# Splitting the second block's first weights ahead, and loading units ahead through the regular weight tiles

## The chip, the cores and the metric

The kernel runs on one core of one Trainium2 chip. The metric is the device time of one execution in microseconds (us), the median of several runs.

## The reference

The input `x` (512 tokens of 1024 features, float32) goes through two blocks of two layers each. Everything is computed in float32.

- A layer of the first block: `x += concat(attention, HGRN, convolution) @ w_out`, where all three get their inputs from `rms_norm(x) @ w_in`; then `x += relu(rms_norm(x) @ w_mlp_in)^2 @ w_mlp_out` with 4096 hidden columns.
- A layer of the second block: `rms_norm(x) @ w_in_2` gives the inputs of four mixers (sparse attention with compressed, selected and window keys; stick-breaking attention; gated linear attention; forgetting attention) and a gate for each. `x += (sum of gate * (mixer @ w_branch_2)) @ w_out_2`; then `x += relu(rms_norm(x) @ w_ff1_2)^2 @ w_ff2_2`.

A last `rms_norm` gives the output. What matters here is that nearly all of the weights (some 16 big matrices) are read once, and that each product is float32.

## The kernel before, in words

**How a product is made.** TensorE takes `fp32r` operands. Each float32 operand is split into a high part `hi` (a rounded copy, made on ScalarE) and a low part `lo = src - hi` (made on VectorE); this is `split`, lines 316 and 317. `mm3` (lines 414 to 416) then makes three matmuls: hi with hi, hi with lo, lo with hi. The activations are split once (`xh`, `xl`); the weights are split as they come.

**How weights come.** A unit of weights is 128 partitions x 512 floats, 256 KB (`units`, line 323). `wload` (line 370) makes one unit after another: SP issues the load of the raw weights into a `wr` tile (line 384), ScalarE writes the high part into `wh`, VectorE the low part into `wl`. These three tags have a fixed number of buffers (line 110), and a tag's buffers are handed out in the order in which the code asks for them:

```python
WEIGHTS = dict(wr=4, wh=4, wl=3)
```

A unit of 512-column products costs TensorE 12 matmuls. `tlater` and `product` use units of 4 x 128 columns, `nlater` (lines 460 to 462) units of 2 x 256 columns.

**Splitting ahead.** `split_ahead` (line 333) takes a list of weights that a later layer will ask for, cuts it into the same units as `wload`, and makes a job of each: load the raw weights into a tile `pr` of its own (line 342), split them into two tiles `pp` of tags that are free at that time, and write both parts to a buffer `parts` in HBM, issued by ScalarE (line 349). `background`, called 64 times in an MLP (after each step of its loops), starts `len(todo) / 64` jobs per call and moves the running ones on by a stage. When `wload` later finds the unit's key among those kept, it loads both parts from HBM straight into `wh` and `wl` (line 379, two transfers of 256 KB on SP); no `wr` tile and no split is used.

Before the change only the MLP of the first block's layer 0 does this: 48 units of layer 1, listed by `First.ahead` (line 1116), with raw tiles of the tag `c` and parts in the tags `hz` and `hx`. The other three MLPs have no jobs.

**The MLP** (`mlp`, line 566) has four chunks of 1024 hidden columns. In each, eight steps make hidden columns (ReLU on ScalarE, line 577; square on GpSimd, line 578; split) and eight steps make output rows (scaling on VectorE, line 588; addition to `x` on GpSimd, line 590). In the last chunk each output row is also prepared for the next layer: `xh` on ScalarE (line 511), `xl` on VectorE (line 512), its square, and the sum of squares on GpSimd (line 505).

**The start of a layer of the second block** (`Second.layer`, line 2099): the first gate column (`G[0][0]`), then `narrow` (line 1485: four groups of 32 columns, among them the forget and gate logits), then `nsa_inputs` (line 1593): two projections of compression keys and values, and `compress` (line 1549), which uses raw weights in `wr` tiles as operands, 8 times two tiles, while units of four `nlater` projections are put between. The queue of other work during the sparse attention (the remaining gates of branch 0 and the first stick-breaking projections) is paced by a credit per step.

**The order of instructions** on each engine and queue is made by the tile framework when the program is built: it takes instructions by program order, but lets a later one go first when its inputs and a buffer are ready by its own timing. So a load that has a free buffer goes out early, and a load that waits for a buffer goes in its turn.

Of the kernel before, what the change touches and what calls it, by code (L numbers as in the profile page):

```python
# [20 lines left out]
F32R = mybir.dt.float32r  # L21
# [10 lines left out]
KT = D // 128  # L32
# [129 lines left out]
class Core:  # L162
# [114 lines left out]
    def ahead(self, work, u):  # L277

        n = work.load(u + 1 + AHEAD - len(work.ws))
        if work in self.queue:  # L280
            for w in self.queue[self.queue.index(work) + 1:]:
                if n <= 0:
                    break
                n -= len(w.ws)
                if n > 0:
                    n = w.load(n)
# [46 lines left out]
    def split_ahead(self, tags, wanted, steps):  # L333


        nc, todo = self.nc, [(u, m, b) for w in wanted for u, m in self.units(*w) for b in (w[2],)]

        def job(unit, m, b):
            view = lambda t: t[:, :m * b].rearrange("p (a b) -> p a b", a=m)
            raw = view(self.t(tags[0], "pr"))  # L340
            for ap, rows, cols in unit:
                nc.sync.dma_start(raw[rows, :, cols], ap)
            yield
            hi, lo = (self.t(tag, "pp", F32R) for tag in tags[1:])
            self.split(view(hi), view(lo), raw)
            yield
            d = self.tc.dram_tile([2, 128, T], F32, name="parts")
            for i, x in enumerate((hi, lo)):
                nc.scalar.dma_start(d[i][:, :m * b], x[:, :m * b].bitcast(F32))
            self.kept[self.unit_key(unit)] = d  # L350

        self.jobs, self.running = [job(*t) for t in todo], []
        self.job_rate, self.job_credit = len(todo) / steps, 0.0
# [443 lines left out]
def weave(core, *gens, until=None):  # L797


    state = [[g, f, t] for g, f, t in gens]  # L800
    need = state[:until]
    while any(st in state for st in need):
        st = min(state, key=lambda a: a[2])
        try:
            st[2] += (next(st[0]) or 1) * st[1]
            core.step()
        except StopIteration:
            state.remove(st)
# [81 lines left out]
class First:  # L890
# [437 lines left out]
    def layer(self, l, gmlp, post):  # L1328
        K, I = self.K, self.I
        w = I["w_out"][l]  # L1330
        cv, hg, at, vi = [], [], [], []
        att = self.att(l, vi, at)
        other = dict(X="hx", near="hx", far="hp", Z="hz", acc="ha")
        slots = [lambda n: K.t(other.get(n, "h"), n), lambda n: K.t(other[n], n) if n in other else K.xtile()]
        K.share, K.pool_share = -8, 1.0
        weave(K, (self.hgrn(l, 0, vi, slots[0], hg), 1, 0), (self.hgrn(l, 1, vi, slots[1], hg), 1, 7),
              (self.conv(l, cv), 2.5, 30), (att, 1, 30), until=3)
        hg = [p for _, p in sorted(hg, key=lambda a: a[0])]
        own = [K.parts(y) for y in cv + hg]
        xs = [self.out_part(w, m, own[2:] + own[:2]) for m in range(KT)]  # L1340
        K.queue_up(xs)
        K.pace(10)
        weave(K, (att, 1, 0))
        K.drain()
        K.pool_share = 0.0
        K.out_proj(w[0:512], [K.parts(y, "h", "hx") for y in at], lambda m: K.prep(m, gmlp()))
        nxt = self.ahead(1) if l == 0 else []
        K.split_ahead(("c", "hz", "hx"), nxt, 64)
        K.mlp(I["w_mlp_in"][l], I["w_mlp_out"][l], post,
              dict(h=[("y", "a")] * 4 + [("y", "h")] * 4, r="t", s="t", o="e", r2="z"))  # L1350

# [3 lines left out]
O_Q, O_KC, O_VC, O_KS = 0, 512, 640, 768  # L1355
O_NG = 1280
O_SB = 1304
O_GQ, O_GK, O_GV, O_GA, O_GG = 2840, 3096, 3352, 3864, 3880
O_FX, O_FF, O_GATE = 4392, 5928, 5936


class Second:
# [111 lines left out]
    def rope(self, v, t, n, p=128):  # L1474
# [6 lines left out]
        nc.vector.tensor_tensor(v[:, :, 0:16], v[:, :, 0:16], C, op=ALU.mult)  # L1481
        nc.vector.tensor_tensor(v[:, :, 0:16], v[:, :, 0:16], b, op=ALU.add)


    def narrow(self, l, other):
        K, nc, I = self.K, self.K.nc, self.I
        w = I["w_in_2"][l]
        ws = K.wload([(w[:, c:c + 32].rearrange("(k p) c -> p k c", p=128), slice(None), slice(32 * i, 32 * i + 32))
                          for i, c in enumerate((O_NG, O_FF, O_GA, O_GA))], KT, 128)
        p = K.pt()  # L1490
        for k in range(KT):
            K.mm3(p, *ws[k], K.xh[k], K.xl[k], k == 0, k == KT - 1)
        z = K.evac(p, "z", name="nar")
        other.get()
        if self.C is None:
            self.constants()

        pg = K.pt("ps")
        for t in range(NT):
            nc.tensor.transpose(pg[:, t * 32:t * 32 + 32], z[0:32, t * 128:(t + 1) * 128], K.ident[0:32, 0:32])  # L1500
        gt = K.small(128, "gates", bufs=1)
        nc.vector.tensor_scalar(gt, pg[:, :128], -40.0, None, op0=ALU.max)
        K.sigmoid(gt, gt)
        gt = gt.rearrange("p (t n) -> p t n", t=NT)
        for t in range(NT):
            nc.vector.tensor_scalar(gt[:, t, 0:24:3], gt[:, t, 0:24:3], self.cmpv[:, t:t + 1], None, op0=ALU.mult)

        bf = K.small(1, "foxb", bufs=1)
        nc.sync.dma_start(bf[32:40], I["fox_b_f_2"][l].rearrange("(p o) -> p o", o=1))
        zf = K.t("e", "zf")  # L1510
        nc.vector.tensor_scalar(zf[32:40], z[32:40], bf[32:40], None, op0=ALU.add)
        ls = K.t("e", "ls")[32:40]
        K.log_sigmoid(ls, zf[32:40])
        cum = K.t("e", "cum")
        nc.vector.tensor_tensor_scan(cum[32:40], K.ones[32:40, 0:1].to_broadcast([8, T]), ls, 0.0, op0=ALU.mult, op1=ALU.add)
        cf = K.bp.tile([128, T], F32R, name="cf", tag="cf")
        nc.vector.tensor_scalar(cf, K.R, 0.0, None, op0=ALU.mult)
        nc.scalar.activation(cf[32:40], cum[32:40], AF.Copy, scale=-1.0)
        nc.vector.scalar_tensor_tensor(cf[0:8], cum[32:40], -1.0, cf[32:40].bitcast(F32), op0=ALU.mult, op1=ALU.subtract)
        nc.gpsimd.tensor_copy(cf[64:128], cf[0:64])  # L1520
        self.low = K.small(T, "low", bufs=1)
        nc.scalar.activation(self.low[0:16], z[64:80], AF.Copy)
        return gt, cf
# [575 lines left out]
    def layer(self, l, gff, post):  # L2099
        K, nc, I = self.K, self.K.nc, self.I  # L2100
        bg = K.vec(I["b_gate_2"][l], "gbias", 32)
        ys = [[] for _ in range(4)]
        mixed = [None] * KT
        G, B = zip(*(self.branch(l, n, ys[n], mixed, bg) for n in range(4)))
        sV, sZ = self.heads_inputs(l, O_SB)
        fV, fZ = self.heads_inputs(l, O_FX)
        g0, g1 = self.gla_inputs(l)
        K.pool_share = 0
        G[0][0].get()
        gt, cf = self.narrow(l, G[0][1])  # L2110
        nin = {}
        K.queue_up(G[0], sV[0], sZ[0], sZ[1])
        K.pace(130 + 18 * 1.2)
        K.pool_share = 0.0
        weave(K, (self.nsa_inputs(l, nin), 1, 0))
        K.pool_share = 0
        weave(K, (self.nsa(gt, nin, ys[0]), 1, 0))
        K.queue_up(sV[1], sZ[2], sZ[3], B[0], G[1], g0["qk"], g0["v"])
        K.pace(56, 40)
        weave(K, (self.stick(sV, sZ, ys[1]), 1, 0))  # L2120
        K.queue_up(g0["g"], g1["qk"], B[1], g1["v"], G[2], g1["g"], fV[0], fZ[0])
        K.pace(24, 20)
        weave(K, (self.gla(l, (g0, g1), ys[2]), 1, 0))
        K.queue_up(fZ[1], fZ[2], B[2], fV[1], fZ[3], G[3])
        K.pace(53, 45)
        weave(K, (self.fox(fV, fZ, cf, ys[3]), 1, 0))
        K.queue_up(B[3])
        K.drain()
        K.pool_share = 0.0
        K.out_proj(I["w_out_2"][l], [K.parts(m, "v") if i < 4 else K.parts(m) for i, m in enumerate(mixed)],  # L2130
                   lambda m: K.prep(m, gff()), kept=True)
        K.mlp(I["w_ff1_2"][l], I["w_ff2_2"][l], post,
              dict(h=[("v", "y")] * 8, r="t", s="t", o="e", r2="q"))

# [58 lines left out]
```

## Time and profile before

| what | us |
|---|---|
| median of 3 runs | 3737.83 |
| the runs | 3732.4 to 3740.15 |
| the profiled execution, its own time | 3730.05 |
| its span, first to last instruction | 3728.3 |

The profile shows one execution. PE is TensorE's matmuls, PEld its weight loads, which overlap them, DVE is VectorE, ACT ScalarE, POOL GpSimd, SP the queue that issues most transfers; a small q behind an engine's name means its sequencer. L317 is line 317 of the kernel. The ends of matmuls are modelled: a stall shorter than a matmul's modelled length shows as busy time. PEclk is the granted clock of TensorE as a share of full speed, DMA the mean busy share of the 16 DMA engines. Where a wait is put down to "issue", the profile shows nothing that the engine waited for.

### The profile page before, as it was taken

The numbers are of one execution on the slowest core, as the hardware profiler recorded it, in microseconds if no ns is written. First come the engines' busy times: TensorE is split into PE (matmuls) and PEld (weight loads), VectorE is DVE, ScalarE is ACT, GpSimd is POOL, SyncE is SP. The second block draws the span as 40 slices with busy tenths as digits, with TensorE's granted clock in tenths as the row PEclk, the third lists the DMA queues.
The fourth block names the chain that finished last, engine by engine and source line by source line (L and its number), as shares of the span: only waits on it lengthen the run. The fifth ranks groups of instructions, "written<-read, shape, count | busy, mean of one in ns | idle before, by whom it ended". The sixth has DMA issues, their size and how long they took to land.

```text
span 3728.3 us, 53465 instructions
## 1 busy us (share of the span) xinstructions
PE 3618.2 (97%) x18793; PEld 3004.0 (81%) x18793; DVE 2322.3 (62%) x4594; ACT 1901.4 (51%) x3940; POOL 892.0 (24%) x885
## 2 busy tenths in 40 slices
PE   8889999998999999999999999999999999999999
PEld 7757788896788887888788888887888888888887
DVE  8885643488543346787778753335687777874334
ACT  6576433356533343678555643333567844553333
POOL 4732222344022230001213122222001121222222
PEclk9999999999999999999999999999999999999999
DMA  4105943541133344213232333334312222233332
GB/s 129 54 12 186 343 132 98 156 132 53 58 96 98 97 119 123 57 46 74 63 74 66 77 113 97 96 98 129 93 32 71 71 66 75 62 105 94 98 97 88
DMA packets 589500, 357.00 MB, mean 96 GB/s; under 512 B 53050, under 2 KB 554416, under 8 KB 589232
## 3 DMA queue, kind: packets, MB, share of 16 engines
q1 hardware_dynamic: 571952, 322.13, 31.1%
q10 hardware_dynamic: 17280, 31.46, 2.2%
q8 instruction: 148, 2.42, 0.3%
q14 instruction: 120, 0.98, 0.1%
HBM read 317.85 MB, written 35.65 MB: 95 GB/s over the span
## 4 chain that ended last, share of the span: by engine, by line
PE 82%; DVE 4%; ACT 2%; DMA 2%; issue 1%; POOL 1%; SPq 0%; ACTq 0%; DVEq 0%; POOLq 0%
PE pm L414 21%; PE pm L416 21%; PE pm L415 21%; PE pm L461 2%; PE pm L462 2%; PE pm L460 2%; PE po L714 2%; PE pt L696 1%; PE pa L1091 1%; PE pt L2041 1%; DVE wl L317 1%; PE ps L2041 1%; PE po L1896 1%; PE ps L1206 1%; DMA wr<-in_w_in_dram 0%
## 5 line engine op out<-in xcount | busy, mean ns | idle before, releaser
L317 DVE TENSOR_TENSOR wl<-wr,wh 128x512 fp32r<-128x512 f32 x948 | 678.5, 716 | 701.5 <-issue 347.8
L316 ACT ACTIVATE wh<-wr 128x512 fp32r<-128x512 f32 x948 | 594.8, 629 | 986.6 <-PE pm L415 825.9
L414 PE MATMUL pm<-xh,wh 128*128 128x512 f32 x2160 | 855.7, 396 | 14.4 <-DVE x L1138 3.8
L416 PE MATMUL pm<-xh,wl 128*128 128x512 f32 x2160 | 850.9, 394 | 4.8 <-POOL wl L389 3.8
L415 PE MATMUL pm<-xl,wh 128*128 128x512 f32 x2160 | 848.1, 393 | 0.2 <-DVE xl L512 0.2
L414 PEld LDWEIGHTS pm<-xh,wh 128*128 128x128 f32 x2160 | 407.8, 189 | 98.9 <-DVE x L1138 4.2
L416 PEld LDWEIGHTS pm<-xh,wl 128*128 128x128 f32 x2160 | 407.6, 189 | 92.9 <-POOL wl L389 5.7
L415 PEld LDWEIGHTS pm<-xl,wh 128*128 128x128 f32 x2160 | 407.6, 189 | 82.0 <-issue 2.2
L416 PE MATMUL pm<-hid,wl 128*128 128x512 f32 x1024 | 398.7, 390 | 2.3 <-DVE wl L317 2.3
L415 PE MATMUL pm<-hid,wh 128*128 128x512 f32 x1024 | 397.9, 389 | 0.0
L414 PE MATMUL pm<-hid,wh 128*128 128x512 f32 x1024 | 396.5, 390 | 0.1
L590 POOL TENSOR_TENSOR x<-x,os 128x512 f32<-128x512 f32 x124 | 205.8, 1660 | 426.7 <-DVE os L588 425.0
L578 POOL TENSOR_TENSOR s<-r 128x512 f32<-128x512 f32 x128 | 134.5, 1051 | 577.5 <-ACT r L577 540.2
L460 PE MATMUL pm<-wh,xh 128*128 128x256 f32 x896 | 257.3, 290 | 6.6 <-ACT wh L316 4.8
L461 PE MATMUL pm<-wl,xh 128*128 128x256 f32 x896 | 257.1, 288 | 2.8 <-DVE wl L317 2.5
L462 PE MATMUL pm<-wh,xl 128*128 128x256 f32 x896 | 255.2, 286 | 0.0
L416 PEld LDWEIGHTS pm<-hid,wl 128*128 128x128 f32 x1024 | 192.2, 188 | 45.0 <-DVE wl L317 5.1
L414 PEld LDWEIGHTS pm<-hid,wh 128*128 128x128 f32 x1024 | 192.2, 188 | 40.2 <-ACT wh L316 0.5
L415 PEld LDWEIGHTS pm<-hid,wh 128*128 128x128 f32 x1024 | 192.2, 188 | 39.8
L414 PE MATMUL pm<-mxh,wh 128*128 128x512 f32 x512 | 202.1, 398 | 6.3 <-ACT mxh L316 4.1
L588 DVE TENSOR_TENSOR os<-pm,R 128x512 f32<-128x512 f32 x128 | 88.5, 692 | 189.7 <-PE pm L416 189.7
L415 PE MATMUL pm<-mxl,wh 128*128 128x512 f32 x512 | 202.0, 394 | 0.0
(621 smaller groups left out, 6698.3 us busy)
## 6 DMA issues: line engine op xcount, KB each, us to landing
wr<-in_w_in_dram SPq DMA_DIRECT2D x344, 256.0 KB
wr<-in_w_ff_dram SPq DMA_DIRECT2D x256, 256.0 KB
wr<-in_w_mlp_in_dram SPq DMA_DIRECT2D x128, 256.0 KB
wr<-in_w_mlp_out_dram SPq DMA_DIRECT2D x128, 256.0 KB
parts<-pp ACTq DMA_DIRECT2D x96, 256.0 KB
wr<-in_w_branch_dram SPq DMA_DIRECT2D x64, 256.0 KB
wr<-in_w_out_dram SPq DMA_DIRECT2D x56, 256.0 KB
wh<-parts SPq DMA_DIRECT2D x48, 256.0 KB
```

Source lines behind the costliest of these rows:

```text
L316: nc.scalar.activation(hi, src, AF.Copy)
L317: nc.vector.tensor_tensor(lo, src, (hi if hi_in is None else hi_in).bitcast(F32), op=ALU.subtract)
L414: nc.tensor.matmul(out, wh, xh, start=start, stop=False)
L415: nc.tensor.matmul(out, wh, xl, start=False, stop=False)
L416: nc.tensor.matmul(out, wl, xh, start=False, stop=stop)
L460: nc.tensor.matmul(o, self.xh[kk][:, c], h, start=f, stop=False, skip_group_check=True)
L461: nc.tensor.matmul(o, self.xh[kk][:, c], l, start=False, stop=False, skip_group_check=True)
L462: nc.tensor.matmul(o, self.xl[kk][:, c], h, start=False, stop=e, skip_group_check=True)
L578: nc.gpsimd.tensor_tensor(s, r, r, op=ALU.mult)
L588: nc.vector.tensor_tensor(s, po, R2, op=ALU.mult)
L590: (nc.vector if last and m == KT - 1 else nc.gpsimd).tensor_tensor(self.x[m], self.x[m], s, op=ALU.add)
L714: nc.tensor.matmul(*x, start=start and n == 0, stop=stop and n == len(mm) - 1, skip_group_check=True)
```

## The change

Three edits. In `split_ahead`, the job's raw tile is a `wr` tile, made by `wtile`, in place of a tile of a tag given by the caller; so the caller gives two tags, those of the parts. In `First.layer`, layer 1 now gives a list as well: that of the second block's layer 0. In `Second.layer`, layer 0 gives the list of layer 1 ahead of its MLP, with parts in the tags `g` and `z`. The new `Second.ahead` lists what a layer of the second block asks for first; `narrow_columns` is the list of `narrow`, taken out of it so that both use the same.

```diff
@@ split_ahead
         def job(unit, m, b):
             view = lambda t: t[:, :m * b].rearrange("p (a b) -> p a b", a=m)
-            raw = view(self.t(tags[0], "pr"))
+            raw = self.wtile("wr", m, b)
             for ap, rows, cols in unit:
                 nc.sync.dma_start(raw[rows, :, cols], ap)
             yield
-            hi, lo = (self.t(tag, "pp", F32R) for tag in tags[1:])
+            hi, lo = (self.t(tag, "pp", F32R) for tag in tags)
             self.split(view(hi), view(lo), raw)
@@ First.layer
-        nxt = self.ahead(1) if l == 0 else []
-        K.split_ahead(("c", "hz", "hx"), nxt, 64)
+        nxt = self.ahead(1) if l == 0 else Second.ahead(K, I, 0)
+        K.split_ahead(("hz", "hx"), nxt, 64)
@@ Second
+    @staticmethod
+    def ahead(K, I, l):
+
+        w = I["w_in_2"][l]
+        out = K.wanted(w, (O_GATE, 128)) + [Second.narrow_columns(w)]
+        out += K.wanted(w, (O_KC, 128), (O_VC, 128), (O_KS, 256), (O_KS + 256, 256), (O_Q, 256), (O_Q + 256, 256))
+        out += K.wanted(w, *((O_GATE + m * 128, 128) for m in range(1, KT)))
+        out += K.wanted(w, (O_SB + 1024, 256), (O_SB, 128), (O_SB + 512, 128), (O_SB + 128, 128), (O_SB + 640, 128))
+        return out + K.wanted(w, (O_SB + 1280, 256), *((O_SB + c, 128) for c in (256, 768, 384, 896)))
+
+    @staticmethod
+    def narrow_columns(w):
+        return [(w[:, c:c + 32].rearrange("(k p) c -> p k c", p=128), slice(None), slice(32 * i, 32 * i + 32))
+                for i, c in enumerate((O_NG, O_FF, O_GA, O_GA))], KT, 128
@@ narrow
-        ws = K.wload([(w[:, c:c + 32].rearrange("(k p) c -> p k c", p=128), slice(None), slice(32 * i, 32 * i + 32))
-                          for i, c in enumerate((O_NG, O_FF, O_GA, O_GA))], KT, 128)
+        ws = K.wload(*self.narrow_columns(w))
@@ Second.layer
+        K.split_ahead(("g", "z"), self.ahead(K, I, 1) if l == 0 else [], 64)
         K.mlp(I["w_ff1_2"][l], I["w_ff2_2"][l], post,
               dict(h=[("v", "y")] * 8, r="t", s="t", o="e", r2="q"))
```

## Rows read from the trace of the kernel before

**Rows 1.** The page: span, busy time by engine, one costly group.

```profile
span 3728.3 us, 53465 instructions
...
PE 3618.2 (97%) x18793; PEld 3004.0 (81%) x18793; DVE 2322.3 (62%) x4594; ACT 1901.4 (51%) x3940; POOL 892.0 (24%) x885
...
L590 POOL TENSOR_TENSOR x<-x,os 128x512 f32<-128x512 f32 x124 | 205.8, 1660 | 426.7 <-DVE os L588 425.0
```

**Rows 2.** Stretches: bounds, length, busy PE PEld DVE ACT POOL, PEclk, DMA share, GB/s.

```profile
356.00:718.00 362.00, 355.26 (x1551) 289.66 (x1550) 173.40 (x250) 144.35 (x249) 95.02 (x70) 1.00 0.60 189
...
1036.00:1386.00 350.00, 350.00 (x1552) 289.65 (x1551) 135.99 (x208) 123.75 (x212) 94.71 (x70) 1.00 0.36 102
1386.00:2197.00 811.00, 796.06 (x4596) 675.57 (x4595) 619.33 (x1456) 480.69 (x1101) 122.72 (x155) 1.00 0.29 77
2197.00:2547.00 350.00, 350.00 (x1551) 289.65 (x1550) 136.21 (x208) 123.94 (x212) 94.34 (x74) 1.00 0.36 104
2547.00:3362.00 815.00, 798.40 (x4596) 678.43 (x4595) 599.72 (x1340) 481.41 (x1100) 119.90 (x146) 0.99 0.29 75
3362.00:3712.00 350.00, 350.00 (x1551) 289.65 (x1550) 139.52 (x205) 117.96 (x201) 93.30 (x69) 1.00 0.32 93
```

**Rows 3.** Stretches of 50 us around the start of the first MLP.

```profile
310.00:360.00 50.00, 50.00 (x223) 39.79 (x222) 31.62 (x44) 23.70 (x40) 16.21 (x12) 1.00 0.70 213
...
360.00:410.00 50.00, 46.67 (x202) 37.60 (x202) 31.31 (x50) 28.91 (x53) 8.43 (x8) 0.97 1.05 344
410.00:460.00 50.00, 46.59 (x196) 35.78 (x195) 33.70 (x43) 19.43 (x33) 13.35 (x8) 1.00 1.04 349
```

**Rows 4.** Waits of PEld, 356 to 718: us in total, times, longest.

```profile
PEld pm L416 <- DVE wl L317: 7.6, 12, 1.4
PEld pm L414 <- ACT r L577: 3.2, 1, 3.2
```

**Rows 5.** Tiles `pr` and `pp`: ns min/median/max, first and last start in us.

```profile
L342 SPq DMA_DIRECT2D pr<-in_w_in_dram x48: 367/368/1304, 298.4 to 439.2; - x48
...
L317 DVE TENSOR_TENSOR pp<-pr,pp x48: 676/685/1783, 325.3 to 474.1; 128x512 fp32r<-128x512 f32 x48
L342 SPq DMA_DIRECT2D pr<-in_w_out_dram x8: 367/368/725, 441.5 to 464.2; - x8
...
L349 ACTq DMA_DIRECT2D parts<-pp x96: 326/327/1273, 302.7 to 475.2; - x96
```

**Rows 6.** Waits of PEld, 1386 to 1510.

```profile
PEld pm L461 <- DVE wl L317: 3.4, 5, 1.7
PEld pm L460 <- ACT wh L316: 3.2, 3, 2.1
PEld ps L1564 <- DMA wr<-in_nsa_cmp_wv_dram: 1.8, 2, 0.9
```

**Rows 7.** Waits of PEld, 2547 to 3362.

```profile
PEld pm L460 <- ACT wh L316: 3.0, 2, 1.6
PEld ps L1564 <- DMA wr<-in_nsa_cmp_wv_dram: 2.8, 3, 1.3
...
PEld pm L461 <- DVE wl L317: 1.5, 3, 0.6
...
PEld ps L1564 <- DMA wr<-in_nsa_cmp_wk_dram: 1.0, 1, 1.0
```

**Rows 8.** Groups by line, 1386 to 1510: busy us, mean ns, idle before.

```profile
L317 DVE TENSOR_TENSOR wl<-wr,wh 128x512 fp32r<-128x512 f32 x33 | 22.7, 689 | 20.2 <-ACT wh L316 9.7 <-issue 5.0 <-PE pm L461 2.4
L316 ACT ACTIVATE wh<-wr 128x512 fp32r<-128x512 f32 x33 | 20.8, 630 | 41.3 <-DMA wr<-in_w_in_dram 21.5 <-PE pm L415 10.3 <-PE pm L462 5.0
```

**Rows 9.** Waits over the whole span.

```profile
DVE wl L317 <- issue: 347.8, 213, 3.9
```

**Rows 10.** The last chunk of the second MLP as a stretch.

```profile
1343.00:1386.00 43.00, 43.00 (x191) 35.59 (x191) 20.87 (x32) 18.66 (x32) 21.41 (x14) 1.00 0.51 139
```

**Rows 11.** Waits of PEld, 718 to 830, the largest entry.

```profile
PEld ps L1206 <- issue: 2.0, 2, 1.6
```

## The prediction

> **What bounds the kernel now.** I read the busy shares first. TensorE is busy 3618.2 of 3728.3 us, no other engine above 62% [rows 1]: whatever the change moves on VectorE, ScalarE or the queues counts only where TensorE waits for it. So the second view is the stretches. Cut where the first block's attention part, its MLP, and so on begin, the span has eight stretches; the six that matter here stand in [rows 2]. Three of the four MLPs take 350 us with TensorE busy in all of it, at the full granted clock. The MLP of the first block's layer 0 (356 to 718) takes 362 us. It alone now splits weights ahead, so the 48 jobs cost 12.0 us. Its idle time is only 362 - 355.3 = 6.7 us: a short stall also stretches the matmuls around it, which the view counts as busy.
>
> The third view is where in that MLP it happens. The jobs load into tiles of their own and so are not held back: the last `pr` load is issued at 464.2 and the last write of parts at 475.2 us, although the code spreads the jobs over all 64 steps [rows 5]. From 360 to 460 the DMA engines are full (share 1.05 and 1.04, 344 and 349 GB/s) and TensorE idles 3.3 and 3.4 us. From 310 to 360, with jobs already running, the share is 0.70 at 213 GB/s and TensorE idles for nothing [rows 3]. The weight-load queue of TensorE waited 7.6 us for low halves `wl` and once 3.2 us for the ReLU that was behind them on ScalarE [rows 4]: full DMA engines deliver the regular weights late.
>
> The fourth view is the start of both layers of the second block, where the 2 x 62 units lie. There TensorE waits for exactly what the change takes away: 1386 to 1510 us for `wl` 3.4, `wh` 3.2 and for raw compression weights 1.8 [rows 6], 8.4 us in all; in layer 1, 3.0, 2.8, 1.5 and 1.0, 8.3 us [rows 7].
>
> **The change part by part.** *Loading through `wr`.* No instruction is added in the MLP of layer 0. A job's raw tile is now one of the four `wr` buffers, which regular weights take in the same order. A `wr` buffer comes free only when a split into `wh`/`wl` is done, and those come free at TensorE's pace. So jobs can't run ahead by more than a few units: 48 jobs are spread over some 350 us. The burst goes, and most of its 12.0 us. Bounds: gain 0 (the price is per job, wherever it lies) to 12.0. I take 10, since the share then is far nearer to the row of 0.70 than to those above 1.
>
> *62 more jobs in the MLP of layer 1, and 62 in the MLP of the second block's layer 0.* The lists give 2 + 2 (gate column, narrow) + 4 + 8 + 8 (KC/VC, KS, Q) + 14 (gates) + 12 + 12 (stick-breaking) = 62 units, a rate of 62/64 a step. By its keys each is what `wload` asks for later. Per job: on SP one load of raw weights (368 ns to issue; four small ones for each of the two narrow units), on ScalarE a copy of 0.63 us and two issues of parts of 0.33 us, on VectorE a subtraction of 0.69 us [rows 5, 8]. In one MLP that is 62 x 1.29 = 80 us on ScalarE beside 123.8 busy, and 43 us on VectorE beside 136.0, of 350 [rows 2]. Both have room, and TensorE has three split units ahead. Behind a job's parts write, which waits on ScalarE for VectorE's half, stand the next `wh` copies, and TensorE waits for those: a delay under a microsecond, covered by those units. On the DMA engines a job moves 256 KB in and 512 KB out: 62 x 0.786 MB in 350 us is 139 GB/s on top of 102, so 241 GB/s. By the first MLP's 0.60 for 189 GB/s [rows 2] that is an estimated share of 0.77. No row has that share with jobs evenly spread. The nearest below is 0.70 without idle, the nearest above 1.04 with idle [rows 3]. The bounds are 0 and 12.0 / 48 = 0.25 us a job, 15.5 us an MLP. I take 2 each, near the lower row.
>
> *Ends of the three MLPs.* Until now no job ran in a last chunk, where VectorE and GpSimd also prepare the next layer's input. From 1343 to 1386 us VectorE is busy 20.9 us and GpSimd 21.4, together 42.3 of 43 [rows 10]. Before many of the splits VectorE idles although all that the profile knows is ready: 347.8 us in 213 waits, 1.63 us each, about one GpSimd addition of 1.66 us [rows 1, 9]. So the two seem to take turns. Eight more subtractions there are 8 x 0.69 = 5.5 us. If they never overlap, 42.3 + 5.5 is 4.8 us more than the stretch; if they do, nothing. I take 1 us at each of the three ends.
>
> The Trainium skill has a rule here: SBUF — State Buffer, "Summary: rules for kernel authors", says that a VectorE operation with two SBUF inputs and a GpSimd operation reading SBUF fully block one another. By that rule alone the sum would have 4.8 us at each end; by the row's lower bound it has 0. The trace agrees so far as the 1.63 us go.
>
> *Splits and raw loads taken out of the second block's layers.* Each of the 62 units loses its split and its raw load and gains two loads of 256 KB straight into `wh` and `wl`. From 1386 to 1510 VectorE spends 22.7 us and ScalarE 20.8 us on 33 such splits [rows 8]. Off the waits of TensorE that buys nothing, so I count only the waits: 8.4 and 8.3 us. The compression weights also stay in `wr`, which then has four buffers for them alone. Bounds: 0 (the wait comes back under another name) to the 14.9 and 16.6 us that TensorE idles in these two parts as a whole (811 - 796.1 and 815 - 798.4) [rows 2]. I take the named waits in full.
>
> *What is late next.* A kept unit holds a `wh` and a `wl` buffer from its DMA's issue on, and there are four and three. On SP a load that waits for such a buffer holds up all behind it, the compression loads among them, and the compression matmuls wait for those. The first block's layer 1 already lives so: from 718 to 830 the largest entry in the list of the weight-load queue is 2.0 us in two waits, ended by nothing that the profile shows, and no `wh` or `wl` is in that list [rows 11]. Bounds 0 to the full 8.4; I take 1 us a layer. Moving the narrow weights' list into a function and taking the `c` tiles out of use cost nothing: no instruction changes, and no one else waits for a `c` tile in the MLP.
>
> **Sum.** -10 - 8.4 - 8.3 + 2 + 2 + 3 + 2 = -17.7 us. The profiled execution took 3730.05 us, 1.75 beyond its span, so 3712.4 in its own terms. It was quicker than all three timed runs, 7.8 us under their median of 3737.83; on the median's scale the forecast is 3720 us.
>
> **Rivals.** *The price is per job.* Point of decision: the DMA share in the MLPs. Should spread traffic at about 0.77 delay the regular weights as much as the burst did, because a job now also holds one of the four `wr` buffers that they need, then 172 jobs cost 0.25 us each: 12 + 15.5 + 15.5 = 43 us against 12 now, +31. Less 16.7 and plus 2 in the layers that is +16.3: 3754 us, slower. For it: the waits of layer 0 were on `wl`, and the `wr` reserve gets thinner. Against it: at 0.70 nothing idled [rows 3]. Chance 0.15.
>
> *The ends of the MLPs give it back.* VectorE and GpSimd strictly take turns in the last chunks, 3 x 4.8 = 14.4 us in place of 3: -17.7 + 11.4 = -6.3, 3732 us, no change that can be told. For it: the 42.3 of 43 us and the 1.63 us waits. Against it: the same stretch loses nothing on TensorE today, and the splits ahead leave slack. Chance 0.15.
>
> *More than the waits.* If MLP 0 gives back all 12.0 and each second-block part 12 us, because the VectorE chain at its start gets shorter and small stalls go with it, and nothing new is late, the time is 3737.8 - 36 = 3702 us. For it: MLP 0 lost nearly twice its idle time. Against it: much of the idle time there is behind evacuations and softmax. Chance 0.18.
>
> *The change does not do what it says* (keys differ, parts are written and never read): the MLP costs stand alone, above 3738. By reading the code every key matches. Chance 0.02.
>
> **How the numbers follow.** The forecast has 0.50. A measurement of this kernel tells about 0.2%, 7.5 us, from no change, so faster means under 3730.4 and slower over 3745.3. Faster: 0.50 + 0.18 = 0.68; same: 0.15; slower: 0.15 + 0.02 = 0.17. The range runs from just below the gain of 36 us to beyond the case of the ends, with the upper cost bounds of two or three small terms: 3700 to 3742. It leaves out the 0.17.
>
> **What would show it.** Right: all four MLP stretches at 350 to 354 us; writes of parts through the whole of three MLPs instead of ending a third of the way in; no slice with a DMA share near 1; 124 fewer subtractions into `wl` and 124 more into `pp`; waits of `pm L460` and `L461` for `wh` and `wl` gone from the starts of the second block's layers, which take about 8 us less each. Wrong: MLP stretches of 360 us or more, a first wait at the layer starts on the `parts` loads, or the second block's parts unchanged although the splits are gone.

## The result, and the profile after

The changed kernel takes 3787.01 us in the median (3781.07 to 3788.93), the kernel before 3735.43 in the same comparison: a ratio of 1.0134, 95% interval 1.0117 to 1.0152. It is slower by about 50 us, where 17.7 us less were forecast.

These are the stretches of the changed kernel's profiled execution that answer to [rows 2], in the same columns (bounds, length, busy PE PEld DVE ACT POOL, PEclk, DMA share, GB/s). The bounds have moved with the work.

```profile
357.00:709.00 352.00, 350.50 (x1551) 289.46 (x1549) 191.88 (x252) 148.20 (x255) 92.58 (x69) 1.00 0.67 207
1031.00:1409.00 378.00, 361.65 (x1555) 286.71 (x1553) 206.11 (x267) 156.63 (x269) 93.66 (x69) 1.00 0.70 220
1409.00:2223.00 814.00, 797.13 (x4596) 677.72 (x4595) 585.93 (x1398) 447.97 (x1045) 121.95 (x156) 0.99 0.35 98
2223.00:2600.00 377.00, 362.23 (x1550) 285.37 (x1549) 206.49 (x266) 156.04 (x267) 90.57 (x70) 1.00 0.71 221
2600.00:3420.00 820.00, 800.37 (x4596) 679.85 (x4595) 563.88 (x1281) 447.42 (x1043) 121.34 (x150) 0.99 0.34 95
3420.00:3770.00 350.00, 350.00 (x1551) 289.65 (x1550) 139.52 (x205) 118.01 (x201) 93.33 (x69) 1.00 0.32 93
```

Cut at the last matmul of each part, to a tenth of a us: the first MLP fell from 362.0 to 351.8, the two MLPs with 62 jobs rose from 350.0 to 377.2 and 377.3, the second block's layers rose from 811.3 to 814.3 and from 815.2 to 820.1, the first block's layer 1 from 318.0 to 322.4 and the part ahead of it by 1.6. The sum is +58; the spans differ by 57.9. The DMA share in the slow MLPs is 0.70, nowhere near 1.

What TensorE waits for in the second MLP (waits of PEld, 1031 to 1409) is no transfer and hardly a weight:

```profile
PEld pm L414 <- ACT r L577: 17.4, 24, 1.5
PEld pm L414 <- issue: 10.5, 8, 2.1
PEld pm L416 <- DVE wl L317: 2.6, 11, 0.2
```

The largest entry is the ReLU that empties one of its two `pm` banks. The 10.5 us under "issue" have no cause that the profile names; a step further down shows one such wait. The view of the job tile `pp` in the same stretch says what stood ahead. The first three rows are the job's instructions, those under "sat idle" the idle time ahead of them:

```profile
L349 ACTq DMA_DIRECT2D parts<-pp x122: 326/327/743, 1032.6 to 1404.1; - x122
L316 ACT ACTIVATE pp<-wr x61: 631/632/635, 1032.0 to 1402.7; 128x512 fp32r<-128x512 f32 x61
L317 DVE TENSOR_TENSOR pp<-wr,pp x61: 691/693/742, 1032.6 to 1403.4; 128x512 fp32r<-128x512 f32 x61
its engine sat idle before it (us, times) until:
  DMA wr<-in_w_in_dram: 142.0, 61
  ACT pp L316: 127.0, 61
```

ScalarE stood idle 142.0 us ahead of 61 copies, 2.3 us each, until the job's raw weights had landed; VectorE stood idle 127.0 us ahead of the subtractions, waiting for these copies. What comes later in the queue of either engine does not pass such an instruction. A step that makes hidden columns shows it on ScalarE: the job's copy, its two writes of parts, and the ReLU (timeline of the changed kernel; start, duration, engine, and the idle time before):

```profile
1158.47 0.63 ACT L316 ACTIVATE pp<-wr 128x512 fp32r<-128x512 f32 x1 [1.85 <-DMA wr<-in_w_in_dram]
1159.13 1.13 ACTq L349 DMA_DIRECT2D parts<-pp  x2
1160.31 0.60 ACT L577 ACTIVATE r<-pm 128x512 f32<-128x512 f32 x1 [1.20 <-DVE pp L317]
```

The ReLU stands behind the copy and also behind the second write, which waits for VectorE's half: 26 of the 32 ReLUs of this MLP waited for that, 31.3 us in all. A step that makes output rows, on ScalarE, VectorE, SP and TensorE:

```profile
1200.28 0.63 ACT L316 ACTIVATE wh<-wr 128x512 fp32r<-128x512 f32 x1 [0.17 <-issue]
1204.81 0.63 ACT L316 ACTIVATE pp<-wr 128x512 fp32r<-128x512 f32 x1 [3.90 <-DMA wr<-in_w_in_dram]
```

```profile
1200.26 2.38 DVE L317 TENSOR_TENSOR wl<-wr,wh 128x512 fp32r<-128x512 f32 x2
1205.47 0.69 DVE L317 TENSOR_TENSOR pp<-wr,pp 128x512 fp32r<-128x512 f32 x1 [2.83 <-ACT pp L316]
1206.09 0.68 DVE L588 TENSOR_TENSOR os<-pm,R 128x512 f32<-128x512 f32 x1
```

```profile
1200.97 0.37 SPq L342 DMA_DIRECT2D wr<-in_w_in_dram  x1
```

```profile
1206.91 0.47 PE L414 MATMUL pm<-hid,wh 128*128 128x512 f32 x1 [0.66 <-DVE os L588]
```

The raw load is issued at 1200.97, and ScalarE's next instruction is already its copy, which starts at 1204.81. VectorE's scaling of a finished bank (L588) comes behind the subtraction; the matmul that needs this bank then stood still 0.66 us, and its weight load shows 1.05 us under "issue".

### The profile page after: what moved, and what is told of

Read it like the earlier page. It is cut to its first block, busy times and chain, and to the rows that moved or that the text cites. A ratio compares the mean times of both kernels' runs of the same rounds, so it can differ in the third digit from the quotient of the medians.

```text
span 3786.2 us, 53904 instructions
## 1 busy us (share of the span) xinstructions
PE 3640.7 (96%) x18793; PEld 3000.6 (79%) x18793; DVE 2408.8 (64%) x4594; ACT 1901.3 (50%) x3940; POOL 885.3 (23%) x885
## 4 chain that ended last, share of the span: by engine, by line
PE 69%; DMA 12%; DVE 11%; ACT 4%; issue 2%; POOL 1%; SPq 0%; DVEq 0%; ACTq 0%; POOLq 0%
PE pm L414 16%; PE pm L416 16%; PE pm L415 16%; DMA wr<-in_w_in_dram 11%; PE pm L460 2%; PE pm L461 2%; PE pm L462 2%; ACT pp L316 2%; PE po L714 2%; DVE wl L317 2%; DVE cy L1287 1%; PE pt L696 1%; PE pa L1091 1%; PE ps L1206 1%; DVE nm L661 1%
## 5 line engine op out<-in xcount | busy, mean ns | idle before, releaser
L416 PE MATMUL pm<-xh,wl 128*128 128x512 f32 x2160 | 851.6, 394 | 14.5 <-DMA wl<-parts 9.7
L316 ACT ACTIVATE wh<-wr 128x512 fp32r<-128x512 f32 x824 | 505.5, 627 | 523.6 <-PE pm L415 371.8
L414 PEld LDWEIGHTS pm<-xh,wh 128*128 128x128 f32 x2160 | 408.0, 189 | 127.0 <-ACT r L577 23.4
L414 PE MATMUL pm<-hid,wh 128*128 128x512 f32 x1024 | 399.7, 393 | 18.3 <-DVE os L588 11.8
L317 DVE TENSOR_TENSOR pp<-wr,pp 128x512 fp32r<-128x512 f32 x172 | 124.1, 722 | 336.5 <-ACT pp L316 336.5
L316 ACT ACTIVATE pp<-wr 128x512 fp32r<-128x512 f32 x172 | 108.6, 632 | 364.6 <-DMA wr<-in_w_in_dram 354.6
```

Source lines behind the costliest of these rows:

```text
L316: nc.scalar.activation(hi, src, AF.Copy)
L317: nc.vector.tensor_tensor(lo, src, (hi if hi_in is None else hi_in).bitcast(F32), op=ALU.subtract)
L414: nc.tensor.matmul(out, wh, xh, start=start, stop=False)
L416: nc.tensor.matmul(out, wl, xh, start=False, stop=stop)
```

## The experiments

Three theories. **Theory 1:** the job's copy and subtraction wait in their queues for raw weights that have not landed, ahead of the instructions that empty TensorE's banks. **Theory 2:** the jobs' traffic delays the regular weights. **Theory 3:** VectorE and GpSimd take turns, and the added subtractions are too many. Times of parts below are cut at the last matmul of each part.

### One part alone, its opposite, and fewer jobs

Only the first edit; the two new lists are empty:

```diff
-        nxt = self.ahead(1) if l == 0 else Second.ahead(K, I, 0)
+        nxt = self.ahead(1) if l == 0 else []
...
-        K.split_ahead(("g", "z"), self.ahead(K, I, 1) if l == 0 else [], 64)
+        K.split_ahead(("g", "z"), [], 64)
```

> The jobs of layer 0 alone, loaded through wr; the two new lists are empty. In the changed kernel the first MLP took 352 us against 362 before. Theory 1 (a job's copy waits in ScalarE's queue, and its subtraction in VectorE's, for raw weights that have not landed, ahead of the ReLU and the scaling that empty TensorE's banks; it costs only where nearly every step has a job), theory 2 (traffic) and theory 3 (VectorE and GpSimd take turns) all expect the first MLP at about 352 and the other three at 350, the rest as before: some 10 us faster than before, about 3726.

Measured: 3719.11 us, ratio 0.9956 (0.994 to 0.9973). The first MLP takes 353.8, the others 350.0. The median is 14.5 us below the kernel before, of which the first MLP explains 8.2. The loading through `wr` is a gain; the loss is all in the new lists.

All jobs, but the raw tile again one of a tag of its own:

```diff
-            raw = self.wtile("wr", m, b)
+            raw = view(self.t(tags[2], "pr"))
...
-        K.split_ahead(("hz", "hx"), nxt, 64)
+        K.split_ahead(("hz", "hx", "c"), nxt, 64)
...
-        K.split_ahead(("g", "z"),
+        K.split_ahead(("g", "z", "k"),
```

> All 172 jobs, but raw weights in tiles of their own again (tag c in the first block, k in the second), so that loads run ahead of their split. Theory 1: in the MLPs with 62 jobs the waits for raw weights shorten, but the jobs bunch up and the DMA engines fill as they did in the first MLP before (12.0 us for 48 jobs): each of the two about 365, the first 362. Theory 2: the same traffic in a burst costs at least as much, 377 or more. Theory 3: the same work in a shorter time, 377 or more.

Measured: 3772.32 us, 1.0102 (1.0087 to 1.0117). The three MLPs take 361.4, 363.0 and 360.9. ScalarE idles 29.1 us ahead of the 53 copies from 1040 us on, not 142. The burst is back, as two stretches of this run's second MLP show beside one after the burst:

```profile
1095.00:1145.00 50.00, 49.14 (x216) 40.04 (x215) 36.16 (x43) 21.18 (x36) 14.20 (x9) 1.00 1.07 353
1145.00:1195.00 50.00, 47.44 (x201) 36.91 (x200) 30.01 (x42) 28.96 (x50) 8.32 (x8) 1.00 1.07 359
...
1245.00:1295.00 50.00, 50.00 (x222) 41.42 (x221) 18.75 (x29) 18.38 (x32) 11.35 (x10) 1.00 0.33 95
```

So there are two prices: 11 to 13 us for a burst, whether of 48 or 62 jobs, and 27 us for 62 spread jobs that wait. Theories 2 and 3 had both put 377 or more here.

No raw loads: each job splits a resident tile.

```diff
-            raw = self.wtile("wr", m, b)
-            for ap, rows, cols in unit:
-                nc.sync.dma_start(raw[rows, :, cols], ap)
+            raw = view(self.scales[0])
```

> The jobs load no raw weights: each splits a resident tile (the kernel leaves out reading the weights ahead, so the units kept hold other numbers). Copy, subtraction and both writes of parts stay, 62 a time; nothing is left to wait for, and a third of a job's traffic is gone. Theory 1: both long MLPs at 350 to 353, the ScalarE idle time ahead of the copies gone, 50 us faster than the changed kernel. Theory 2: two thirds of the extra traffic stay, so some two thirds of the 27 us each, 368. Theory 3: no change, 377.

Measured: 3741.79 us, ratio 1.0014 (1.0005 to 1.0024). The second MLP took 350.4, as theory 1 expects, with all 62 copies, subtractions and writes in it. The third took 369.2, close to the 368 of theory 2. With nothing to hold them back the jobs bunched in both, at 1045 to 1166 and at 2208 to 2329 us. Here are the two MLPs, and 50 us out of each bunch:

```profile
1026.00:1376.00 350.00, 350.00 (x1550) 289.53 (x1549) 180.24 (x266) 155.26 (x269) 95.66 (x70) 1.00 0.60 195
1076.00:1126.00 50.00, 50.00 (x222) 41.44 (x221) 38.09 (x52) 25.77 (x45) 14.42 (x9) 1.00 1.00 339
2189.00:2558.00 369.00, 357.89 (x1551) 289.01 (x1550) 181.86 (x267) 156.50 (x269) 96.31 (x74) 1.00 0.57 187
2239.00:2289.00 50.00, 42.57 (x167) 31.07 (x166) 33.67 (x44) 25.24 (x43) 12.43 (x8) 0.97 0.97 342
```

The first of these speaks against theory 3, since the same VectorE work cost nothing. The second shows that full DMA engines (share 1.00, 339 GB/s) alone need not cost TensorE anything. In the third MLP TensorE waited 10.4 us for `wh` and 8.2 for `wl`, but the `wh` copies themselves waited only 0.5 us for raw weights; the jobs' copies stood 18.8 us on ScalarE until an earlier job's subtraction was done (11.9 in the second MLP). So its loss is not one of late raw weights; why it came there and not in the second MLP stays open. And as the traffic had changed with the waiting, theory 2 is not yet excluded for the changed kernel.

The lists cut to 48 and, later, to 55 units:

```diff
-for b in (w[2],)]
+for b in (w[2],)][:48]
```

> The two new lists cut to their first 48 units, 0.75 jobs a step as in the first MLP; otherwise the changed kernel. Theory 1: a step's ScalarE and VectorE time with the wait then fits in the 5.4 us on average, as in the first MLP: both long MLPs 352 to 355. Theory 2 and theory 3, in proportion to the jobs: 350 + 27 x 48/62 = 371 each. The layers of the second block say whether units kept ahead gain anything there: 811 and 815 before, 814 and 820 in the changed kernel.

> The two new lists cut to 55 units, 0.86 jobs a step. At 48 units these MLPs took 352 and 350, at 62 they took 377. Theory 1 in its form with a threshold (per step ScalarE's or VectorE's work, waits included, against 5.4 us of TensorE's): a few us, 353 to 364. If something else lies between 48 and 62 units, such as what the last 14 units are, it could be all or nothing: 350 or 375.

Measured with 48: 3728.48 us, 0.998 (0.9971 to 0.999), the two MLPs at 352.2 and 350.3; the second block's layers at 811.9 and 817.2. With 55: 3756.22, 1.006 (1.0045 to 1.0075), the two at 365.5 and 367.9, a little above what theory 1 gave. It is neither a price per job nor all or nothing. ScalarE's idle time ahead of the copies in the second MLP was 86, 116 and 142 us with 48, 55 and 62 jobs; the MLP lost 2, 16 and 27.

### The order alone

One rule on the order, nothing else: a job's copy stands behind the last weight copy traced before it on ScalarE, its subtraction behind the last one on VectorE. Below this is called the late split.

```diff
-            self.split(view(hi), view(lo), raw)
+            on_act, on_dve = self.last
+            with self.tc.issue_after(on_act), self.tc.issue_after(on_dve):
+                self.split(view(hi), view(lo), raw)
```

(`self.last` holds the two instructions of the last split in `wload`.)

> The changed kernel with one rule more on the order: a job's copy stands behind the last weight copy traced before it on ScalarE, its subtraction behind the last weight subtraction on VectorE, so that both come one step of the MLP later than the framework puts them. All 172 jobs, all traffic and all work stay. Theory 1 (the wait in the queue): the raw weights have landed by then; ScalarE's idle time ahead of the 61 copies falls from 142 us to under 40, and the two long MLPs take 350 to 354 instead of 377, the whole some 48 us less, about 3735. Theory 2 (traffic) and theory 3 (turns of VectorE and GpSimd): 377 as before.

Measured: 3726.41 us, 0.9977 (0.9968 to 0.9986); the two MLPs at 350.0 and 351.4. Here is the tile `pp` in the second MLP, with its idle times, and then the two MLPs as stretches:

```profile
L316 ACT ACTIVATE pp<-wr x62: 612/616/634, 1032.9 to 1378.9; 128x512 fp32r<-128x512 f32 x62
L317 DVE TENSOR_TENSOR pp<-wr,pp x62: 676/684/1781, 1036.0 to 1379.5; 128x512 fp32r<-128x512 f32 x62
its engine sat idle before it (us, times) until:
  DMA wr<-in_w_in_dram: 0.6, 1
  ACT pp L316: 0.3, 1
```

```profile
1033.00:1383.00 350.00, 350.00 (x1551) 289.36 (x1549) 188.34 (x266) 157.11 (x268) 87.08 (x69) 1.00 0.78 236
2198.00:2550.00 352.00, 351.44 (x1552) 289.56 (x1550) 189.32 (x267) 157.14 (x268) 87.34 (x73) 1.00 0.79 237
```

Same jobs, same bytes, same work, and in less time, so at a higher share (0.78 against 0.70). 142.0 us of waiting ahead of the jobs' copies became 0.6, and the 27 us are gone. Theories 2 and 3 fall as the cause of these 27 us. The thinner reserve of `wr` buffers falls too: over the last 40 jobs of the second MLP a job held its buffer 10.2 us in the median from the issue of its load to its subtraction, against 4.6 in the changed kernel.

That the place of the job's split in the queues costs the 27 us is shown. Waiting on a transfer as such is not the price, as ScalarE's waits in the second MLP of this run show:

```profile
ACT wh L316 <- DMA wr<-in_w_mlp_out_dram: 79.4, 48, 4.0
ACT wh L316 <- DMA wr<-in_w_mlp_in_dram: 52.6, 49, 3.6
ACT r L581 <- PE pm L420: 14.8, 19, 1.2
```

ScalarE now waits 132.0 us ahead of the regular copies for their raw weights, and loses nothing by it: the ReLU (here line 581) waits for TensorE alone. In the chunks after the first, ReLUs follow one another at 5.8 to 6.0 us on average in the changed kernel, and mostly at 5.44 with the late split, which is TensorE's own pace (24 matmuls of 227 ns). The edit took away two waits ahead of the ReLU, the copy's for its raw weights and the write's for VectorE's half, and one ahead of the scaling; what each of them cost by itself was not tried.

For the version with the first block's jobs alone, the rule gives nothing to be told:

> Only the first block's 48 units, through wr, with the late split and three wl buffers. ScalarE's idle time ahead of the copies (84 us in the first MLP) goes, the MLP falls from 353.8 to 351, and the rest stays: 3716 against 3719.

Measured: 3720.09 us, 0.9963 (0.995 to 0.9977), against 3719.11 without it. The first MLP did fall to 350.0.

### The second block's layers

With clean MLPs the layers still gained nothing: 815.8 and 818.7 with the late split, against 810.6 and 814.9 in the run just named, which loads them as regular weights. These are single profiles, the first of that version's slowest execution and the second of the other's quickest; the medians lie 6.3 us apart. Over all profiles with three buffers, the smaller pad of the next attempt left out, the layers took 811.9 to 821.8 and 812.9 to 820.1 with 48 to 62 kept units, 810.6 to 811.3 and 811.5 to 815.2 with regular weights. At their starts TensorE now waits for parts (waits of PEld in the changed kernel, 1400 to 1540, in place of [rows 6]):

```profile
PEld pm L416 <- DMA wl<-parts: 4.8, 2, 2.8
...
PEld pm L461 <- DMA wl<-parts: 0.9, 1, 0.9
```

and SP stands with the load of parts in hand until a weight buffer is free (SP's own waits, same stretch):

```profile
SPq L379 <- PE pm L416: 36.0, 15, 7.3
SPq L379 <- PE pm L462: 18.4, 13, 3.1
```

The suspicion: with three `wl` buffers, a kept low half is asked for only when a buffer comes free, and then needs a transfer, where a regular one needs 0.69 us on VectorE. The test is a fourth buffer, with a control that loads the second block's units as regular weights. It took three attempts, since the room for it moves other tiles. The controls of the first two attempts also lack the late split, which acts on jobs alone, and so not in these layers.

```diff
-WEIGHTS = dict(wr=4, wh=4, wl=3)
+WEIGHTS = dict(wr=4, wh=4, wl=4)
...
-        self.pad(self.core_w, 96)
+        self.pad(self.core_w, 64)
```

> The kernel with the late split and four wl buffers in place of three (a pad of 96 bytes is cut to 64 for the room). It is for the layers of the second block, which gained nothing in the changed kernel (814 and 820 against 811 and 815) although 62 splits left each. If the loads of kept parts, which wait for one of three wl buffers, took the gain (waits of 5 us on wl at the start of each), the two layers now take some 5 to 8 us less each than with three buffers. If the layers don't depend on weights at all, they stay at 814 and 818.

> The jobs of the first MLP alone, through wr (3719 us), with four wl buffers and the smaller pad: the control for the run with four buffers. If the buffer helps regular weights too, the second block's layers (811 and 812) take less here as well, 3 us or more each; if it helps kept parts alone, they stay.

Measured: 3743.32 us (1.0024, 1.0014 to 1.0034) and, for the control, 3773.49 (1.0106, 1.0091 to 1.0121). Both are slower than with three buffers, and even the last MLP, without jobs, takes 355.2. Against its control the version with kept units has layers of 812.6 and 816.0 where the control has 823.5 and 822.5. The pad alone explains the slow MLPs, with three buffers and the first block's jobs only:

> Only the first block's 48 units, through wr, three wl buffers, and only the pad of the weight tiles cut from 96 to 64 bytes. If the pad made the matmuls on xh and xl go from 227 to 234 ns in the runs with four buffers, they do so here: MLPs without jobs at 355 instead of 350, the whole some 50 us slower than with 96 bytes. If it was the fourth buffer, 227 ns and 3719.

Measured: 3747.36 us (one run), all MLPs without jobs at 355.2. In its last MLP the matmuls on `xh` and `xl` have grown, those on the hidden columns have not:

```profile
L414 PE MATMUL pm<-xh,wh 128*128 128x512 f32 x185 | 73.1, 395 | 0.0
...
L415 PE MATMUL pm<-hid,wh 128*128 128x512 f32 x178 | 69.2, 389 | 0.0
```

From one start to the next that is 234 ns in the median in place of 227, at the same granted clock (1.00). The cost of the pad was 28 us, about half of what I had put.

Second attempt: the pad at 96 again, 32 bytes taken from the first block's own pad (160 to 128).

> Late split and four wl buffers once more, with the room taken from a pad of the first block's own tiles (160 to 128 bytes) and the pad of the weight tiles left at 96. The claim: with three wl buffers, kept parts cost the layers what they save; with four they save about 9 us a layer. Then the MLPs stay at 350 to 352, the second block's layers take some 803 and 808 instead of 816 and 819, and the whole some 3705 to 3712. If the gain of the last run with four buffers against its control came from the layout alone, 3726 as with three.

> The control: only the first block's 48 units, through wr, with the same four wl buffers and the same pads. Regular weights need 0.7 us for a low half after a buffer comes free and no transfer, so a fourth buffer gives them little: layers of the second block at 811 and 812 as with three, the whole at 3717 to 3722. If the fourth buffer helps all weights, some 3710.

Measured: 3720.14 (0.9963, 0.9953 to 0.9974) and 3751.4 (1.0044, 1.0031 to 1.0057). The layers are at 808.5 and 808.8 against 816.5 and 812.9. Now the first block's hidden columns were the slow operand (234.5 ns; its MLPs 355), and the second block was clean. In the control the 48 jobs of the first MLP waited 131 us on ScalarE, and that MLP took 373.0: 18 us more than with the late split, at 0.75 jobs a step. So the number of jobs a step does not decide; with the first split, 48 jobs cost 4 us where they waited 84 us and 18 where they waited 131.

Third attempt: the first block's pad from 160 to 32, both with the late split.

> All 172 jobs, late split, four wl buffers, room taken from the first block's pad by 128 bytes (160 to 32), so that tiles keep their offset modulo 128. If the offset between a matmul's weights and its moving operand made 227 into 234 ns, all MLPs are at 350 to 352 again. The second block's layers at 808 and 809 as in the last run with four buffers, against 816 and 819 with three: the whole at 3707 to 3714. If kept units gain nothing in the layers with clean offsets either, 3720 or more.

> The control: the same buffers, pads and late split, but only the first block's 48 units ahead; the second block's layers load regular weights. If kept units with four buffers are worth something, its layers take longer than those of the run beside it by 4 to 8 us each, 812 to 817; the whole at 3717 to 3722. If the fourth buffer alone made the layers faster, they are the same, 808 and 809.

Measured: 3720.5 (0.9964, 0.9952 to 0.9977) and 3739.0 (1.0014, 1.0005 to 1.0023). The layers, with kept units first, then with regular weights:

```profile
1387.00:2192.00 805.00, 792.16 (x4599) 673.68 (x4598) 581.74 (x1399) 448.69 (x1044) 120.69 (x156) 1.00 0.35 99
2543.00:3352.00 809.00, 794.15 (x4595) 675.13 (x4596) 564.58 (x1282) 447.81 (x1043) 119.20 (x146) 1.00 0.35 98
```

```profile
1385.00:2200.00 815.00, 796.17 (x4596) 674.71 (x4595) 615.29 (x1457) 481.64 (x1100) 121.10 (x155) 1.00 0.29 76
2550.00:3368.00 818.00, 801.84 (x4600) 679.76 (x4599) 606.27 (x1342) 482.35 (x1102) 121.67 (x146) 0.99 0.29 75
```

Kept units are worth 10.6 and 7.7 us there, once four buffers hold their low halves. TensorE's waits for parts in these layers are 1.6 and 0.9 us, against 6.1 and 6.0 in the changed kernel. The guess on the offset failed: the first block's MLPs were still at 355.

Last, again with all 172 jobs, the late split and four `wl` buffers: the room from a tile of the convolution that was wider than its use, all pads as before:

```diff
-            u = K.gp.tile([128, T + 64], F32, name="u", tag="cu", bufs=1)[:, :T + 30]
+            u = K.gp.tile([128, T + 32], F32, name="u", tag="cu", bufs=1)[:, :T + 30]
```

> All 172 jobs, late split, four wl buffers, all pads as in the kernel before; the room comes from the convolution's padded tile (576 to 544 columns, of which 542 are used). If the MLPs of the first block return to 350 to 352 (matmuls on the hidden columns at 227 instead of 232 ns) and the second block's layers stay at 804 to 810, the whole takes 3708 to 3714, less than any version so far. If the offset of the hidden columns is still a slow one, 3720.

Measured: 3710.66 us (3708.89 to 3714.37), 0.994 (0.9926 to 0.9954), the fastest version here: 23 us below the kernel before. Its stretches, first, second and third MLP and both layers of the second block:

```profile
356.00:707.00 351.00, 351.00 (x1551) 289.83 (x1551) 188.53 (x251) 145.10 (x254) 94.61 (x69) 1.00 0.70 209
1028.00:1379.00 351.00, 350.80 (x1549) 289.14 (x1548) 193.08 (x265) 151.79 (x269) 87.88 (x69) 1.00 0.80 236
1379.00:2187.00 808.00, 794.18 (x4596) 676.26 (x4597) 581.45 (x1398) 448.59 (x1044) 120.64 (x156) 1.00 0.35 99
2187.00:2537.00 350.00, 350.00 (x1551) 289.75 (x1549) 194.07 (x266) 152.88 (x268) 87.13 (x72) 1.00 0.81 238
2537.00:3345.00 808.00, 794.09 (x4596) 674.14 (x4595) 564.29 (x1282) 447.89 (x1043) 119.49 (x148) 1.00 0.35 98
```

## Why the prediction was wrong

**Loading through `wr`: right.** Forecast -10, measured -10.2. The burst ended, the jobs spread over the whole MLP (parts are written until its end), and no stretch of some 50 us had a share above 0.74, where two had been at 1.05 and 1.04. That full DMA engines were the reason of the loss is not shown: without raw loads a share of 1.00 cost nothing.

**62 jobs in an MLP: wrong, 2 us forecast, 27 measured, twice.** The step that failed is this: "Behind a job's parts write, which waits on ScalarE for VectorE's half, stand the next `wh` copies, and TensorE waits for those: a delay under a microsecond, covered by those units." It had the wrong followers, and left out a wait. Behind the write stands not only the next `wh` copy, for which units are in reserve, but in most steps the ReLU, and behind the subtraction the scaling; TensorE has only two `pm` banks to cover these. The wait for VectorE's half was 1.2 us, ahead of 26 of 32 ReLUs. The wait that was put at nothing is that of the copy for its raw weights, 2.3 us each, 142.0 us in an MLP, and of the subtraction behind it. In the kernel before, ScalarE waited 8.5 us in all for `pr` loads ahead of its 48 copies, because a tile of its own was loaded long ahead; the `wr` buffer that ends the burst also brings the load close to its use. The busy times that I summed (80 and 43 us in 350) were right and beside the point, since they say nothing of the order. The text ahead of the prediction says that the framework orders by its own timing, and I drew the consequence for the loads alone.

**Traffic: right.** The estimated share of 0.77 came out as 0.78 and 0.79 with the late split, with TensorE idle for 0 and 0.6 us. **Ends of the MLPs: too dear.** With jobs in the last chunks the MLPs take 350.0 and 351.4, so the rival that gave 3732 falls too. The rule of the Trainium skill on VectorE and GpSimd (SBUF — State Buffer, "Summary: rules for kernel authors") may hold there, but no run shows that it costs TensorE anything.

**The second block's layers: wrong, -14.7 forecast, +7.9 measured.** The waits for `wh` and `wl` from a split did go. The step that failed is "I take 1 us a layer" for what is late next: in the place of the named 8.4 and 8.3 us TensorE waits 6.1 and 6.0 us for parts and still 1.3 and 1.4 for compression weights, 7.4 us a layer. It rested on the first block's layer 1, whose list held no such wait. What makes the layers longer than before, beyond that, was not found. With four `wl` buffers the same units gain 18.3 us against their control, close to the 16.7 put for the waits. Against three buffers and regular weights (810.6 and 814.9) 11.4 us of that is left, since the control with four buffers has 815.1 and 817.3, and 9.1 us in the fastest version. Whether and why regular weights do worse with a fourth buffer was not tried.

**The rivals.** The direction was that of "the price is per job", but not its mechanism: spread traffic costs nothing with the late split, nor does the longer hold on `wr` buffers, and 48 spread jobs cost 0 to 4 or 16 to 18 us, by where their splits stand. Its 15.5 us an MLP were also too few, since its price was taken from a burst.

## What to carry to other kernels

When a transfer's buffer is shared to slow it down, look at which instruction waits for the transfer and what stands behind it in the same engine's queue. Neither busy nor waiting time decides: here 142 us of waiting ahead of the jobs' copies cost 27 us, and 132 us ahead of regular copies nothing. Where a framework orders by its own timing, pin the consumer of a late load behind work that is known to come later. And a part loaded ready-made holds its buffer from the issue of the load; here it paid only with a fourth buffer, where one made on the spot had done with three.

## What the runs showed of the hardware

A matmul of 128x512 from `xh` or `xl` took 227 ns from start to start, and 234 when the pad of the weight tiles was cut by 32 bytes; those on the hidden columns, with the same weight tiles, stayed at 227. They slowed alone when the first block's own pad was cut (median 234.5 ns with 32 bytes less, 232 with 128, mean 233.3 in both; the fourth buffer came in beside it). With 256 columns of weights as the moving operand it was the other way round: 120 ns, and 117 with the smaller pad. The granted clock was 1.00 in the MLPs compared here. 32 bytes of padding were worth 28 us of the whole, in one run. As each operand slowed with the other's matmuls unchanged, it seems to be the distance between the two operands' tiles that decides; which distance is slow, and why, stays open.

DMA engines with a share of 1.00 (339 GB/s) left TensorE busy in all of 50 us in the run without raw loads; in stretches at 0.97 to 1.07 of other MLPs it idled 0.9 to 7.4 us.
